# One encoder layer on one core: gate/up results split into halves as they are made, and a last block of 448 and 128 tokens

## The chip, the core and the metric

The kernel runs on one core of one Trainium2 chip. The metric is device time in microseconds (us). Before the change, three runs gave a median of 2537.41 us (2534.61 to 2539.2). The engines are TensorE (PE; its weight loads are listed apart as PEld), VectorE (DVE), ScalarE (ACT), GpSimd (POOL) and SyncE (SP), which here issues the DMAs of the stages that matter.

## What is computed

One layer of a streaming encoder on 576 tokens (64 of a running stream, 512 of a new one), width 2048, feed-forward width 5632, in float32. Attention and its projections come first and are not touched. What follows, cut from the reference:

```python
x = x + mix @ lp['w_out']
h = rmsnorm(x, lp['norm_ffn_g'])
x = x + (jax.nn.silu(h @ lp['ffn_w_gate']) * (h @ lp['ffn_w_up'])) @ lp['ffn_w_down']
...
y_prompt = rmsnorm(xp[:, N_META:], final_norm_g)
y_sample = rmsnorm(xs, final_norm_g)
```

`rmsnorm` multiplies by 1/sqrt(mean(x*x) + 1e-6) and a gain.

## The kernel before

**Numbers.** Every float32 operand v is split into hi, a copy rounded to a faster matmul format (fp32r), made on ScalarE, and lo = v - hi, made on VectorE. A product is three matmuls: hi x hi, hi x lo, lo x hi. In the trace `wh`, `wl` are the halves of a weight tile and `bh`, `bl` those of an operand; almost all instructions of ScalarE and VectorE are recorded under line 125, through which they are issued.

**Seven products.** `winograd` (line 1068) multiplies a 2 x 2 arrangement of weight tiles by a 2 x 2 arrangement of operand quarters (128 rows x 288 tokens) with seven products instead of eight. Four of the seven weights are sums of tiles (`ws`, made by GpSimd at line 1095 or by VectorE); likewise operands 3 to 7 of a chunk are partly sums of quarters. Each product takes the first two kinds of matmul (line 1126) over all its chunks, then the third kind (line 1130). `take` then adds the PSUM bank into the result. `WIDE` and `CHAIN` (lines 1010 and 1012) are orders of the seven products; `step` is a hook called after each.

**Gate/up stage** (line 1280). 22 steps u, one per 256 columns of the feed-forward width, each a gate pass and an up pass of 7 products x 24 matmuls of 128 x 288. ScalarE applies silu (`gated`), GpSimd multiplies gate and up into w, computes four sums of its quarters, and SP stores w to `actspill` and the sums to `sumspill` in HBM.

**Down stage** (line 1428). The 22 chunks are consumed in `blocks` of 4, 4, 4, 4, 4 and 2. For each of the first five, eight column groups d of 256 output columns run `down_rows` (line 1358): one 1 MB weight load `raw` (two buffers), seven products of 12 matmuls in the order `CHAIN`, results added into the residual rows y0 to y15, which are loaded from `x2spill` two at a time in block 0. While a block runs, `builder` (line 1228) loads the next block's quarters, 144 KB each, four ahead, and splits each: a copy `bh` on ScalarE, a subtraction `bl` on VectorE, 28 of each for a block, 8 for the last. The first block's operands are loaded and split by the same builder in the last steps of the last up pass.

**Last block** (2 chunks, 8 operands, no sums). Two halves of 288 tokens; in each, eight column groups load their weights (512 KB), split them and multiply (`plain_rows`, line 1338; its matmuls are recorded at line 205). `squares` (line 1372) squares each finished y on GpSimd and accumulates (lines 1376 to 1380), and ScalarE scales y by the final gain. `finish` (line 1383) sums the squares over partitions by a matmul with ones (line 1406), takes the reciprocal root, transposes y back on TensorE (line 1394), multiplies, and stores twelve groups `ot`; the first half's runs between the column groups of the second, the second half's at the end.

SP issues loads and stores in one queue, in the order in which the scheduler placed them; a transfer whose buffer is not free holds up those behind it.

Of the kernel before, what the change touches and what calls it, by code (L numbers as in the profile page):

```python
# [2 lines left out]

# [128 lines left out]
def encoder_step(  # L132
# [196 lines left out]
    sumspill = dp.tile([FC // 2, P, 4, QH], F32, name="sumspill")  # L329
    mspill = dp.tile([KC, P, TQ], F32, name="mspill")  # L330
# [673 lines left out]
    rb2 = rw.tile([P, TQ], F32, name="rb2")  # L1004
    sq2 = rw.tile([P, TQ], F32, name="sq2")
# [13 lines left out]

    def operand(m, p, src):  # L1020
        hi = bc.tile([P, QH], F32R, name=f"bh{p}_{m}")
        lo = bc.tile([P, QH], F32R, name=f"bl{p}_{m}")
        pin(S.activation(hi, src, AF.Copy))
        pin(V.tensor_tensor(lo, src, f32(hi), op=ALU.subtract))
        operands[m, p] = (hi, lo)
# [41 lines left out]

    def winograd(wpool, spool, raws, slots, take, banks=None, engine=V, step=lambda: None, stag=("ws", 3),
# [10 lines left out]
        def split_weights(n, srcs):  # L1079
            wh = wpool.tile([P, n, P], F32R, name="wh", tag="wh", bufs=2)  # L1080
            wl = wpool.tile([P, n, P], F32R, name="wl", tag="wl", bufs=2)
# [104 lines left out]
    close_ma()  # L1186
    fb, close_fb = pool("fb", "right")


    def stile():  # L1190
        return fr.tile([P, QH], F32, name="s", tag="s", bufs=4)

    def combined(c11, c12, c21, c22, chain):
# [15 lines left out]
        def take(p, banks):  # L1209
            if p == 1:  # L1210
                s[1] = stile()
                S.activation(s[1], banks[1], AF.Copy)
            elif p == 6:
                s[2] = stile()
# [13 lines left out]
    def builder(m0, count, plain, ahead, by_product=False):  # L1228

        srcs = {}  # L1230
        for m in range(m0, m0 + count):
            quarter = [actspill[2 * m + f, :, c] for f in range(2) for c in (slice(0, QH), slice(QH, TQ))]
            if plain:
                for p, src in zip((1, 2, 4, 5), quarter):
                    srcs[m, p] = src
            else:
                for p, src in zip(ORDER, (quarter[0], quarter[2], sumspill[m, :, 2], sumspill[m, :, 0],
                                          sumspill[m, :, 1], quarter[3], sumspill[m, :, 3])):
                    srcs[m, p] = src
        order = [p for p, _ in CHAIN]  # L1240
        todo = sorted(srcs, key=lambda mp: order.index(mp[1])) if by_product else list(srcs)

        def fetch(n):
            for m, p in todo[n:n + 1]:
                hi = bc.tile([P, QH], F32R, name=f"bh{p}_{m % 8}")
                lo = bc.tile([P, QH], F32R, name=f"bl{p}_{m % 8}")
                load(f32(lo), srcs[m, p])
                operands[m % 8, p] = (hi, lo)

        for n in range(ahead):  # L1250
            fetch(n)
        for n, (m, p) in enumerate(todo):
            fetch(n + ahead)
            hi, lo = operands[m % 8, p]
            pin(S.activation(hi, f32(lo), AF.Copy))
            yield
            pin(V.tensor_tensor(lo, f32(lo), f32(hi), op=ALU.subtract))
            yield
# [17 lines left out]

    turn = 0
    norm = token_norm()
    start = builder(0, blocks[0], False, 4, True)
    for u in range(FC // 2):  # L1280
        out = {}
        for which, wsrc in (("g", w_gate), ("u", w_up)):
# [9 lines left out]
            take = combined(*quarters(c[:, 0, :], c[:, 1, :]), chain)  # L1292
            done = [0]

            def step():
                if u == 0 and which == "u":
                    next(norm, None)
                if u == FC // 2 - 1 and which == "u":
                    done[0] += 1
                    if done[0] > 2:  # L1300
                        for _ in range(2 * blocks[0]):
                            next(start, None)

            if first:
                winograd(fw, fb, raws, range(4, 8), take, banks0, step=step)
            else:
                winograd(fw, fb, raws, range(8), take, step=step, chain=chain)
# [4 lines left out]
        if u == 0:  # L1312
            gated(g)
        for f in range(2):
            G.tensor_tensor(w[:, f, :], w[:, f, :], g[:, f, :], op=ALU.mult)
            if u < FC // 2 - 1:
                store(actspill[2 * u + f], w[:, f, :])
        if u < FC // 2 - blocks[-1]:
# [6 lines left out]
            store(sumspill[u], t)  # L1325
    for _ in start:
        pass
    for f in range(2):
        store(actspill[FC - 2 + f], out["u"][:, f, :])
    close_fb()  # L1330
    close_rw()
    yy, close_yy = pool("yy", "right")
    close_fw()
    yp, close_yp = pool("yp")

    y = []

    def plain_rows(m0, n, d, hs, slots, done):

        banks = {(f, h): pmt()[:, 0:QH] for f in range(2) for h in hs}  # L1340
        r = load_raw(fr, w_down, m0 * 256, 2 * n, d * 256, 2)
        for g in range(0, n, 2):
            for f in range(2):
                wh = yp.tile([P, 4, P], F32R, name="wh", tag="wh", bufs=2)
                wl = yp.tile([P, 4, P], F32R, name="wl", tag="wl", bufs=2)
                split(wh, wl, r[:, 2 * g:2 * g + 4, f * P:(f + 1) * P])
                for k in range(4):
                    m = slots[g + k // 2]
                    ops = [operands[m, ((1, 2), (4, 5))[k % 2][h]] for h in hs]
                    mm3([banks[f, h] for h in hs], wh[:, k, :], wl[:, k, :], [o[0] for o in ops],  # L1350
                        [o[1] for o in ops], g + k == 0, g + k == n + 1)
        for f in range(2):
            for h in hs:
                c = y[2 * d + f][:, h * QH:(h + 1) * QH]
                V.tensor_tensor(c, c, banks[f, h], op=ALU.add)
                done(2 * d + f, h)

    def down_rows(m0, n, d, slots, step):
        raws = [load_raw(fr, w_down, m0 * 256, 2 * n, d * 256, 2)]
        y11, y12, y21, y22 = quarters(y[2 * d], y[2 * d + 1])  # L1360
# [6 lines left out]
        winograd(yp, yp, raws, slots, take, step=step, chain=CHAIN)  # L1367

    tok = [[(0, NS), (NS, P), (192, 96)], [(QH, P), (416, P), (544, 32)]]
    sqs = {}  # L1370

    def squares(i, h):
        c = y[i][:, h * QH:(h + 1) * QH]
        if i == 0:
            sqs[h] = stile()
            G.tensor_tensor(sqs[h], c, c, op=ALU.mult)
        else:
            t = stile()
            G.tensor_tensor(t, c, c, op=ALU.mult)
            G.tensor_tensor(sqs[h], sqs[h], t, op=ALU.add)  # L1380
        S.activation(c, c, AF.Copy, scale=gE[:, i:i + 1])

    def finish(h, ahead):
# [4 lines left out]
        groups = [(q, j) for q in range(4) for j in range(3)]  # L1388

        def turned(q, j):  # L1390
            o, n = tok[h][j]
            ps = pmt()
            for k in range(4):
                PE.transpose(ps[0:n, k * P:(k + 1) * P], y[q * 4 + k][:, o:o + n], ident)
# [7 lines left out]
        vc = yp.tile([P, 3], F32, name=f"vc{h}")  # L1402
        rc = yp.tile([P, 3], F32, name=f"rc{h}")
        V.memset(vc, 1.0)
        for j, (o, n) in enumerate(tok[h]):
# [128 lines left out]
```

## Time and profile before

| | us |
|---|---|
| median of 3 runs | 2537.41 |
| the profiled execution | 2533.22 |
| its span | 2531.3 |
| attention | 0 to 853 |
| output projection | 853 to 970 |
| gate/up | 970 to 1961.9 |
| down, blocks 0 to 4 (with the step into it) | 1961.9 to 2447.1 |
| last block and outputs | 2447.1 to 2531.3 |

The profile shows the profiled execution alone, and its times are counted from the span's start; the time of that execution is 1.92 us longer than the span. Busy times are sums over instructions. Matmuls overlap, so the pace of TensorE is read from the starts of successive matmuls or from a stretch in which it never waits. In the lists of waits, "A <- B" says that A was held up by B. "PEclk" or granted clock is the TensorE clock as a share of full speed.

### The profile page before, as it was taken

Reading aid. Unit: us, or ns where it says so; the run is one execution under the profiler, and the core shown is the slowest. Engines: PE = TensorE matmul, PEld = TensorE weight load, DVE = VectorE, ACT = ScalarE, POOL = GpSimd, SP = SyncE. Lnnn points to the kernel's source line nnn. Section 1 sums busy time; section 2 is a strip of 40 time slices with the busy share of each in tenths; the row PEclk is TensorE's granted clock in tenths of the full one; section 3 lists DMA queues with packets and bytes.
Section 4 is the critical chain, followed back from the end, with each engine's and each line's share of the span. In section 5 each row is a group of like instructions: output and inputs, shape, how many; then the busy total and the mean of one; then the engine's idle time right before and its main releaser. Section 6 shows DMA issues by size and latency. Waiting matters only on the chain. (4 is left out here: it accounts for less than half of the span.)

```text
span 2531.3 us, 44872 instructions
## 1 busy us (share of the span) xinstructions
PE 2440.7 (96%) x17847; PEld 2381.8 (94%) x17847; DVE 1800.2 (71%) x2826; ACT 1106.6 (44%) x2008; POOL 744.3 (29%) x621
## 2 busy tenths in 40 slices
PE   8999999989999999999999999999999899999997
PEld 6999999988999888999999999999999899999997
DVE  5555555556555568877777777777777899999975
ACT  5343333333433444444444444444445444444445
POOL 0000000010000265644545454454543222222236
PEclk9999999999999999999999999999999899999999
DMA  7432232334322553333433333333335642542334
GB/s 216 141 93 80 81 87 83 82 111 120 100 84 76 166 151 112 125 126 121 137 109 117 117 125 132 119 125 100 128 128 167 207 150 84 159 157 84 111 100 150
DMA packets 330116, 307.73 MB, mean 122 GB/s; under 512 B 24708, under 2 KB 298507, under 8 KB 329907
## 3 DMA queue, kind: packets, MB, share of 16 engines
q1 hardware_dynamic: 329346, 302.80, 38.3%
q8 instruction: 140, 2.29, 0.4%
q0 software_dynamic: 560, 2.06, 0.2%
q14 instruction: 70, 0.57, 0.1%
HBM read 250.82 MB, written 56.68 MB: 121 GB/s over the span
## 5 line engine op out<-in xcount | busy, mean ns | idle before, releaser
L1126 PE MATMUL m<-bh,wh 128*128 128x288 f32 x3584 | 968.0, 296 | 11.0 <-DMA bl<-sumspill 8.4
L1126 PE MATMUL m<-bl,wh 128*128 128x288 f32 x3584 | 967.5, 295 | 0.0
L1126 PEld LDWEIGHTS m<-bh,wh 128*128 128x128 f32 x3584 | 673.9, 188 | 11.8 <-ACT wh L125 11.7
L1126 PEld LDWEIGHTS m<-bl,wh 128*128 128x128 f32 x3584 | 677.4, 189 | 0.1
L1130 PE MATMUL m<-bh,wl 128*128 128x288 f32 x3584 | 585.5, 298 | 17.1 <-DVE wl L125 14.5
L1130 PEld LDWEIGHTS m<-bh,wl 128*128 128x128 f32 x3584 | 512.2, 188 | 30.6 <-DVE wl L125 30.1
L1095 POOL TENSOR_TENSOR ws<-raw 128x512 f32<-128x512 f32 x256 | 344.1, 1352 | 599.1 <-DVE wl L125 319.2
L125 ACT ACTIVATE wh<-ws 128x512 fp32r<-128x512 f32 (+1 forms) x340 | 288.8, 849 | 447.6 <-PE m L1126 296.8
L125 DVE TENSOR_TENSOR wl<-ws,wh 128x512 fp32r<-128x512 f32 (+1 forms) x340 | 378.8, 1114 | 114.3 <-ACT wh L125 114.3
L125 DVE TENSOR_TENSOR wl<-raw,wh 128x512 fp32r<-128x512 f32 x416 | 403.7, 984 | 26.1 <-ACT wh L125 16.8
L125 ACT ACTIVATE wh<-raw 128x512 fp32r<-128x512 f32 x416 | 249.7, 626 | 306.2 <-PE m L1126 279.9
L108 PE MATMUL ps<-xh,wh 128*128 128x296 f32 x960 | 221.4, 312 | 1.2 <-ACT wh L125 1.2
L108 PE MATMUL ps<-xh,wl 128*128 128x296 f32 x960 | 210.7, 301 | 1.2 <-DVE wl L125 1.2
L108 PE MATMUL ps<-xl,wh 128*128 128x296 f32 x960 | 210.5, 301 | 0.0
L108 PEld LDWEIGHTS ps<-xh,wh 128*128 128x128 f32 x960 | 157.1, 191 | 5.5 <-ACT wh L125 1.7
L108 PEld LDWEIGHTS ps<-xh,wl 128*128 128x128 f32 x960 | 157.0, 190 | 2.2 <-DVE wl L125 2.2
L125 DVE TENSOR_TENSOR y<-y,m 128x288 f32<-128x288 f32 x312 | 139.6, 447 | 27.2 <-PE m L1130 18.0
L108 PEld LDWEIGHTS ps<-xl,wh 128*128 128x128 f32 x960 | 157.5, 190 | 0.0
L125 DVE TENSOR_TENSOR ws<-ws,raw 128x512 f32<-128x512 f32 x128 | 92.3, 722 | 83.6 <-POOL ws L1095 77.2
L125 DVE TENSOR_TENSOR wl<-wr,wh 128x1024 fp32r<-128x1024 f32 (+1 forms) x110 | 117.7, 1070 | 36.9 <-ACT wh L125 35.4
L125 ACT ACTIVATE wh<-wr 128x1024 fp32r<-128x1024 f32 (+1 forms) x110 | 101.7, 929 | 61.8 <-PE ps L108 52.0
L1273 POOL TENSOR_TENSOR c<-c,rb 128x576 f32<-128x576 f32 x44 | 73.2, 1664 | 164.8 <-ACT c L125 162.3
(359 smaller groups left out, 3342.5 us busy)
## 6 DMA issues: line engine op xcount, KB each, us to landing
raw<-in_ffn_w_gate SPq DMA_DIRECT2D x44, 1024.0 KB, 6.9
raw<-in_ffn_w_up SPq DMA_DIRECT2D x44, 1024.0 KB, 5.9
raw<-in_ffn_w_down SPq DMA_DIRECT2D x40, 1024.0 KB, 5.4
wr<-in_w_in SPq DMA_DIRECT2D x60, 512.0 KB, 4.0
actspill<-c SPq DMA_DIRECT2D x44, 288.0 KB, 2.1
sumspill<-c SPq DMA_DIRECT2D x20, 576.0 KB, 2.8
bl<-sumspill SPq DMA_DIRECT2D x80, 144.0 KB, 3.5
bl<-actspill SPq DMA_DIRECT2D x68, 144.0 KB, 3.9
```

The lines of the kernel that those rows point to most:

```text
L108: self.tc.keep_in_program_order(self.pe.matmul(out, lhsT, rhs, start=start, stop=stop))
L125: ins = issue(*args, **kwargs)
L1095: engine.tensor_tensor(w[:, k:k + m, :], pick(xs), pick(ys), op=op)
L1126: PE.matmul(banks[p], wh[:, k, :], x, start=first and new and k == 0 and x is hi, stop=False, skip_group_check=not new)
L1130: PE.matmul(banks[p], wl[:, k, :], hi, start=False, stop=last and k == n - 1, skip_group_check=not new)
L1273: G.tensor_tensor(g[:, f, :], g[:, f, :], rb2, op=ALU.mult)
```

## The change

1. **Gate/up.** For u = 2 to 19 nothing goes to `actspill` or `sumspill`. In the steps of u + 1 (the last three of the gate pass, the first four of the up pass) `parts` splits each of the chunk's seven operands: a one-column ScalarE copy into the tile's first column, whose source is a column of the result that the product just ended has produced; the hi copy over the whole tile; the lo subtraction on VectorE; and one store of both halves (288 KB) to `partspill`. Chunks 0 and 1 (`WHOLE`) and the last two are stored as before.
2. **Down.** `fetch_parts` loads both halves of an operand with one 288 KB load, and nothing is split in blocks 0 to 3 but the operands of chunks 0 and 1, which `starter` splits in the last up pass and at its end. Block 4 still splits the last block's 8 operands. Weight pools of gate/up and down are one, with four tiles of each half in flight in the down stage instead of two.
3. **The step into the down stage.** The first weights, y0 and y1 are requested from the last up pass on (SP in program order there), the last gate x up multiplication is done by quarters on GpSimd, y2 to y4 take a buffer of gate/up's weights, and y5 to y15 are all requested in the first block's second column group.
4. **Last block.** Its tokens are cut into part 0 (448: 288 and 160) and part 1 (128). Weights are loaded and split once and kept. Squares are taken by ScalarE; GpSimd only accumulates them, and not part 1's last three. `finish` of part 0 makes 20 output groups between part 1's column groups; that of part 1 makes 4.

How it moves instructions, at three places. First ScalarE in the gate/up stage, in the second half of a gate pass: `c<-m` takes a product's result, `wh` are copies of weights to come. Before:

```order
785 L125 ACTIVATE wh<-raw 128x512
786 L125 ACTIVATE wh<-ws 128x1024 x2
787 L125 ACTIVATE c<-m 128x288
788 L125 ACTIVATE wh<-ws 128x1024
789 L125 ACTIVATE c<-m 128x288
790 L125 ACTIVATE wh<-ws 128x1024
```

Now:

```order
885 L125 ACTIVATE c<-m 128x288
886 L125 ACTIVATE parts<-c 128x1
887 L125 ACTIVATE parts<-c 128x288
888 L125 ACTIVATE wh<-ws 128x1024
889 L125 ACTIVATE c<-m 128x288
890 L125 ACTIVATE parts<-c 128x1
891 L125 ACTIVATE parts<-c 128x288
892 L125 ACTIVATE wh<-ws 128x1024
893 L125 ACTIVATE c<-m 128x288
894 L125 ACTIVATE wh<-raw 128x512 x6
```

Ahead of the weight copies at these places stand a one-column copy and a hi copy.

Second, VectorE in the third block of the down stage, in the fifth column group (its rows of y are `y_22271`, `y_22273` before and `y_22248`, `y_22250` now). Before:

```order
2006 L125 TENSOR_TENSOR y_22271<-y_22271,m 128x288
2007 L125 TENSOR_TENSOR wl<-ws,wh 128x512
2008 L125 TENSOR_TENSOR y_22273<-y_22273,m 128x288
2009 L125 TENSOR_TENSOR bl_6_24528<-bl_6_24528,bh_6_24527 128x288
2010 L125 TENSOR_TENSOR wl<-raw,wh 128x512
2011 L125 TENSOR_TENSOR y_22271<-y_22271,m 128x288
2012 L125 TENSOR_TENSOR wl<-ws,wh 128x512
2013 L125 TENSOR_TENSOR ws<-ws,raw 128x512
2014 L125 TENSOR_TENSOR y_22271<-y_22271,m 128x288
2015 L125 TENSOR_TENSOR bl_6_24573<-bl_6_24573,bh_6_24572 128x288
```

Now:

```order
2043 L125 TENSOR_TENSOR y_22248<-y_22248,m 128x288
2044 L125 TENSOR_TENSOR y_22250<-y_22250,m 128x288
2045 L125 TENSOR_TENSOR wl<-ws,wh 128x512 x2
2046 L125 TENSOR_TENSOR y_22248<-y_22248,m 128x288
2047 L125 TENSOR_TENSOR ws<-ws,raw 128x512
2048 L125 TENSOR_TENSOR y_22248<-y_22248,m 128x288
```

The subtractions `bl` are gone from between the weight halves and the additions into y.

Third, SP in block 0, up to the weights of the third column group (`raw_21968` before, `raw_22396` now). Before:

```order
577 L125 DMA y4_21964<-x2spill_68 128x576
578 L125 DMA y5_21966<-x2spill_68 128x576
579 L125 DMA y6_22119<-x2spill_68 128x576
580 L125 DMA y7_22121<-x2spill_68 128x576
581 L125 DMA bl4_6_22207<-sumspill_70 128x288
582 L125 DMA y8_22271<-x2spill_68 128x576
583 L125 DMA y9_22273<-x2spill_68 128x576
584 L125 DMA bl6_6_22296<-sumspill_70 128x288
585 L125 DMA bl3_6_22340<-actspill_69 128x288
586 L125 DMA bl7_6_22382<-sumspill_70 128x288
587 L125 DMA bl1_7_22423<-actspill_69 128x288
588 L125 DMA raw_21968<-in_ffn_w_down 128x8x256
```

Now:

```order
660 L125 DMA y8_22248<-x2spill_68 128x576
661 L125 DMA y9_22250<-x2spill_68 128x576
662 L125 DMA y10_22252<-x2spill_68 128x576
663 L125 DMA y11_22254<-x2spill_68 128x576
664 L125 DMA y12_22256<-x2spill_68 128x576
665 L125 DMA y13_22258<-x2spill_68 128x576
666 L125 DMA y14_22260<-x2spill_68 128x576
667 L125 DMA y15_22262<-x2spill_68 128x576
668 L125 DMA b3_4_22280<-partspill_71 128x576
669 L125 DMA b2_5_22377<-partspill_71 128x576
670 L125 DMA b4_5_22394<-partspill_71 128x576
671 L125 DMA raw_22396<-in_ffn_w_down 128x8x256
```

All remaining rows y, and whole operands in place of quarters, now stand ahead of these weights.

The diff, cut to its core:

```diff
+    def weight_tiles(wpool, n):
+        if n == 8 or not spare:
+            both = [wpool.tile([P, 8, P], F32R, name=x, tag=x, bufs=2) for x in ("wh", "wl")]
+            if n == 8:
+                return both
+            spare.append([w[:, 4:8, :] for w in both])
+            return [w[:, 0:4, :] for w in both]
+        return spare.pop()
...
+    def fetch_parts(m, p):
+        load(f32(operand_tile(m % 8, p)), partspill[m, :, PIECE[p]])
+
+    def fetcher(m0, count):
+        n = 0
+        for m in range(m0, m0 + count):
+            for p in ORDER:
+                fetch_parts(m, p)
+                yield
+                n += 1
+                if n % 2 == 0:
+                    yield
...
+    def starter():
...
+        todo = [p for p, _ in CHAIN]
+        for i in range(len(todo) + 2):
+            if i < len(todo):
+                for m in range(blocks[0]):
+                    if m < WHOLE:
+                        fetch_whole(m, todo[i], whole(m, todo[i]))
+                    else:
+                        fetch_parts(m, todo[i])
+            if i > 1:
+                for m in range(WHOLE):
+                    split_in_place(m, todo[i - 2])
+            yield
...
+    WHOLE = 2
+
+    def parts(u, srcs):
+        for p in ORDER:
+            b = fb.tile([P, 2, QH], F32R, name="parts", tag="parts", bufs=2)
+            S.activation(b[:, 0, 0:1], (yield), AF.Copy)
+            S.activation(b[:, 0, :], srcs[PIECE[p]], AF.Copy)
+            V.tensor_tensor(b[:, 1, :], srcs[PIECE[p]], f32(b[:, 0, :]), op=ALU.subtract)
+            store(partspill[u, :, PIECE[p]], f32(b))
+        yield
...
             def step():
...
+                done[0] += 1
+                if pieces and (which == "u" or done[0] > 4):
+                    try:
+                        pieces.send(took[WIDE[done[0] - 1][0]][:, 0:1])
+                    except StopIteration:
+                        pieces = None
+                if ending:
+                    next(start)
...
-            store(sumspill[u], t)
+            if u < WHOLE:
+                store(sumspill[u], t)
+            else:
+                pieces = parts(u, [b11, b12, b21, b22] + [t[:, i, :] for i in range(4)])
+                next(pieces)
...
+    LATE = TQ - P
+    spans = [[(0, 0, QH), (1, 0, LATE - QH)], [(1, LATE - QH, QH)]]
...
+    def plain_weights(m0, n, d):
         r = load_raw(fr, w_down, m0 * 256, 2 * n, d * 256, 2)
+            kept[d, f] = wh, wl = [room(names, F32R)[:, 0:4 * P].rearrange("p (k c) -> p k c", k=4) for _ in range(2)]
+            split(wh, wl, r[:, :, f * P:(f + 1) * P])
...
+    def squares(i, part):
+        alone = i == 0 or part and i > KC - 4
+        t = room(names if alone else sums)
+        for c, at in token_pieces(i, part):
+            S.activation(t[:, at], c, AF.Square)
+            S.activation(c, c, AF.Copy, scale=gE[:, i:i + 1])
...
-                    for i in (2 * d, 2 * d + 1):
-                        y.append(yy.tile([P, TQ], F32, name=f"y{i}"))
-                        load(y[i], x2spill[i])
+                if bi == 0 and d == 1:
...
+                    for i in range(6, KC):
+                        accumulator(i, yy.tile([P, TQ], F32, name=f"y{i}"))
...
+            for d in range(KC // 2):
+                plain_weights(first, n, d)
+                plain_rows(d, 0, slots)
+            before = finish(0, 0)
+            for d in range(KC // 2):
+                plain_rows(d, 1, slots)
+                for _ in range(3):
+                    next(before, None)
+            for g in (before, finish(1, 4)):
+                for _ in g:
+                    pass
```

More of the change, by code (lines that the diff above doesn't have):

```diff
@@ L1 @@
+import itertools
 import math
@@ L1079, in split_weights @@
         def split_weights(n, srcs):
[L1080 to L1081 removed]
+            wh, wl = weight_tiles(wpool, n)
             k = 0
@@ new lines, in fetch_whole, with act_quarter, whole @@
+    def fetch_whole(m, p, src):
+        operand_tile(m % 8, p)
+        load(f32(operands[m % 8, p][1]), src)
+    def act_quarter(m, q):
+        return actspill[2 * m + q // 2, :, q % 2 * QH:(q % 2 + 1) * QH]
+    def starter():
+        def whole(m, p):
+            q = PIECE[p]
+            return act_quarter(m, q) if q < 4 else sumspill[m, :, q - 4]
+        todo = [p for p, _ in CHAIN]
[10 more added lines that the diff above has]
+            yield
@@ new lines, in plain_rows @@
+    def plain_rows(d, part, slots):
+        for f in range(2):
+            wh, wl = kept[d, f]
+            outs = [pmt()[:, 0:b - a] for _, a, b in spans[part]]
+            for k in range(4):
+                ops = [[x[:, a:b] for x in operands[slots[k // 2], ((1, 2), (4, 5))[k % 2][h]]]
+                       for h, a, b in spans[part]]
+                mm3(outs, wh[:, k, :], wl[:, k, :], [o[0] for o in ops], [o[1] for o in ops], k == 0, k == 3)
+            for c, pi in zip(token_pieces(2 * d + f, part), outs):
+                V.tensor_tensor(c[0], c[0], pi, op=ALU.add)
+            squares(2 * d + f, part)
@@ L1365, in take, with room, finish @@
                 V.tensor_tensor(c, c, banks[p], op=ALU.add)
[L1367 to L1376, printed above, removed]
-        else:
[L1378 to L1388, printed above, removed]
+        winograd(fw, fs, raws, slots, take, step=step, chain=CHAIN)
+    tok = [[(0, 96), (96, 96), (192, 96), (QH, 80), (QH + 80, 80)], [(LATE, P)]]
+    sqs = [[], []]
+    def room(names, dtype=F32):
+        return bc.tile([P, 2, QH], dtype, name=next(names)).rearrange("p a b -> p (a b)")
+    def squares(i, part):
[4 more added lines that the diff above has]
+            S.activation(c, c, AF.Copy, scale=gE[:, i:i + 1])
+        w = slice(0, P if part else LATE)
+        if alone:
+            sqs[part].append(t)
+        else:
+            G.tensor_tensor(sqs[part][0][:, w], sqs[part][0][:, w], t[:, w], op=ALU.add)
+    def finish(part, ahead):
+        groups = [(q, j) for q in range(4) for j in range(len(tok[part]))]
         def turned(q, j):
-            o, n = tok[h][j]
+            o, n = tok[part][j]
+            h = o // QH
             ps = pmt()
             for k in range(4):
-                PE.transpose(ps[0:n, k * P:(k + 1) * P], y[q * 4 + k][:, o:o + n], ident)
+                PE.transpose(ps[0:n, k * P:(k + 1) * P], y[q * 4 + k][h][:, o - h * QH:o - h * QH + n], ident)
             return ps
@@ L1444, in encoder_step @@
         else:
[L1445 to L1454 removed]
+            rest = [m for m in range(8) if m not in slots]
+            free = [f"b{p}_{m}" for m in rest[::-1][:2] for p in ORDER]
+            free += [f"b{p}_{m}" for m in slots for p in (3, 6, 7)]
+            free += [f"b{p}_{m}" for m in rest[:-2] for p in ORDER]
+            sums, free = itertools.cycle(free[0:3]), free[3:]
+            names, rows = iter(free[:-6]), itertools.cycle(free[-6:])
+            for d in range(KC // 2):
[9 more added lines that the diff above has]
+                    pass
         first += n
[L1456 removed]
+    close_fs()
+    close_fw()
     close_fr()
     close_yy()
+    close_rw()
     close_bc()
```

184 lines of the change are left out of this document (94 added, 90 removed).

## The prediction

> **What bounds the kernel now.** I began with the page's busy times, then cut the span into stages by windows, then asked what TensorE waits for in each. The page, and the windows of the four stages that the change touches (times from the span's start; columns: length, then busy time and recorded instructions of each engine, granted clock, DMA share, GB/s):
>
> ```profile
> span 2531.3 us, 44872 instructions
> PE 2440.7 (96%) x17847; PEld 2381.8 (94%) x17847; DVE 1800.2 (71%) x2826; ACT 1106.6 (44%) x2008; POOL 744.3 (29%) x621
> ...
> 1105.00:1910.00 805.00, 805.00 (x6053) 805.00 (x6052) 601.79 (x685) 352.54 (x541) 399.33 (x289) 1.00 0.36 121
> ...
> 1970.40:2068.70 98.30, 94.97 (x672) 92.37 (x673) 89.69 (x156) 45.67 (x86) 23.22 (x18) 0.96 0.51 166
> 2068.70:2164.10 95.40, 92.39 (x675) 89.61 (x674) 89.54 (x157) 44.90 (x85) 21.12 (x16) 1.00 0.42 132
> ...
> 2259.50:2355.70 96.20, 92.12 (x674) 89.55 (x674) 88.15 (x157) 44.73 (x85) 20.70 (x16) 1.00 0.37 115
> 2355.70:2447.10 91.40, 90.53 (x674) 89.34 (x673) 80.59 (x137) 37.56 (x64) 18.95 (x14) 1.00 0.30 92
> 2355.70:2404.00 48.30, 47.55 (x353) 46.70 (x352) 44.78 (x78) 20.83 (x37) 10.79 (x8) 1.00 0.33 99
> 2404.00:2447.00 43.00, 42.87 (x322) 42.55 (x321) 35.81 (x61) 16.62 (x27) 8.16 (x6) 1.00 0.27 84
> 2447.10:2513.50 66.40, 60.68 (x436) 56.65 (x435) 43.03 (x75) 38.38 (x71) 52.39 (x59) 1.00 0.49 149
> 2513.50:2531.30 17.80, 8.36 (x60) 6.89 (x57) 5.79 (x13) 8.71 (x13) 2.21 (x3) 0.80 0.42 147
> ```
>
> In gate/up (first window) TensorE never stops: 805.00/6053 = 0.133 us per matmul, with VectorE at 75%. A down block of 672 matmuls at that pace is 89.4 us, but the full blocks take 95.40 to 96.20 us, and there VectorE is busy 92 to 94%. In block 4 the operand splits stop half way; from 2404 on TensorE keeps its pace (43.00/322 = 0.134). So VectorE gates the first four blocks. The waits of TensorE (us in total, times, longest), from 970 to 2446, then from 2068.7 to 2447:
>
> ```profile
> PE m L1130 <- DVE wl L125: 14.5, 27, 1.5
> PE m L1126 <- DMA bl<-sumspill: 8.4, 1, 8.4
> ...
> PE m L1130 <- DVE wl L125: 9.3, 19, 0.7
> ```
>
> The one long wait is the step into the down stage. TensorE's timeline there, and the traffic around it:
>
> ```profile
> 1960.78 1.23 PE L1130 MATMUL m<-bh,wl 128*128 128x288 f32 x8
> 1970.45 0.61 PE L1126 MATMUL m<-bh,wh 128*128 128x288 f32 x1 [8.43 <-DMA bl<-sumspill]
> 1970.86 0.44 PE L1126 MATMUL m<-bl,wh 128*128 128x288 f32 x1
> 1971.10 0.44 PE L1126 MATMUL m<-bh,wh 128*128 128x288 f32 x1
> ...
> 1945.00:1970.00 25.00, 17.02 (x128) 16.78 (x127) 21.05 (x41) 15.86 (x37) 4.83 (x4) 0.88 0.93 288
> 1970.00:1980.00 10.00, 8.66 (x41) 8.32 (x42) 6.58 (x11) 3.88 (x8) 3.70 (x3) 0.61 0.93 310
> 1990.00:1995.00 5.00, 5.00 (x39) 5.00 (x39) 4.37 (x9) 2.29 (x5) 1.89 (x2) 1.00 1.07 390
> ```
>
> Gate/up ends at T = 1961.9; after 8.43 us of idling the matmuls come every 0.24 us, and the mean clock of 0.61 over 10 us means (1 - 0.61)/0.5 x 10 = 7.8 us at half speed, which costs 3.9 us.
>
> **The change part by part.** Sums are made against the profiled execution (span 2531.3 us, time 2533.22 us), 4.2 us under the median of 2537.41 us; the same difference is then applied to the median. About 0.2% (5 us) can be told from no change.
>
> *Blocks 1 to 3.* Their 28 splits each leave this stage. The rows of the splits and of their neighbours (busy, mean ns):
>
> ```profile
> L125 DVE TENSOR_TENSOR bl<-bl,bh 128x288 fp32r<-128x288 f32 x126 | 83.8, 667 | 3.0 <-ACT bh L125 3.0
> L125 ACT ACTIVATE bh<-bl 128x288 fp32r<-128x288 f32 x124 | 53.0, 429 | 7.8 <-DMA bl<-sumspill 7.6 <-DMA bl<-actspill 0.2
> L125 DVE TENSOR_TENSOR y<-y,m 128x288 f32<-128x288 f32 x312 | 139.6, 447 | 27.2 <-PE m L1130 18.0 <-PE m L205 7.7
> L125 DVE TENSOR_TENSOR wl<-raw,wh 128x512 fp32r<-128x512 f32 x152 | 130.2, 857 | 12.6 <-ACT wh L125 12.2
> ```
>
> VectorE loses 28 x 0.667 = 18.7 of 89.5 us a block, which leaves 74% of today's 95.40; and there are four weight tiles instead of two to run ahead in. What is late next is TensorE itself. 95.40, 95.40 and 96.20 become 3 x 89.4 + 0.8 = 269.0: 287.0 to 269.0, -18.0 (-12 if half of the loss had another cause, -19 with no wait left). Each fetch doubles to 288 KB, so a block reads 28 x 147 KB = 4.1 MB more: 132 GB/s becomes 132 + 4.1 MB/95.4 us = 175, well under what the step into the stage moved.
>
> *Gate/up.* 18 chunks x 7 operands add 126 subtractions on VectorE, 126 copies and 126 one-column copies on ScalarE, 126 stores on SP; the actspill and sumspill stores go. By the rows of the subtractions beside (0.447 to 0.667 us) VectorE gets 56 to 84 us more in 18 chunks: in the window above 601.79 becomes about 672, 84%. TensorE's pace hides it as long as the next weights' low halves arrive: a product lasts 24 x 0.133 = 3.19 us, and its low half is needed only after 16 of 24 matmuls. The new wait is in ScalarE's queue: a one-column copy waits for the result of the product just ended, and behind it stand the weight copies of the products to come. But this wait ends at a point at which TensorE has only begun the next product, whose weights are already split. I take +1 (0 to +8); without that cover it is a rival.
>
> *Transition and block 0.* Before, T to the end of block 0 took 106.8 us. Operands of m = 2, 3 now arrive split, those of m = 0, 1 in the order of use with two products of lead, and the first weights are requested before T. So the 8.43 us wait and its slow clock go: I take 0.5. But SP's order has a new risk. After T it must move product 4's operands (864 KB), raw 1 (1024), y2 to y4 (864), two stores (576), five operands (1440), y5 to y15 at once (3168), three operands (864), and only then raw 2 (1024): 9824 KB = 10.06 MB. Before, raw 2 stood behind y0 to y9 and half-size fetches, and was issued 14.3 us into the block; the other two rows are the landing of such a load and the first copy that needs it:
>
> ```profile
> 1984.78 0.38 SPq L125 DMA_DIRECT2D raw<-in_ffn_w_down  x1
> ...
> raw<-in_ffn_w_down SPq DMA_DIRECT2D x40, 1024.0 KB, 5.4
> ...
> L125 ACT ACTIVATE wh<-raw 128x512 fp32r<-128x512 f32 x152 | 95.6, 630 | 109.0 <-PE m L1126 91.6 <-DVE wl L125 8.8 <-DMA raw<-in_ffn_w_down 3.7
> ```
>
> At 339 GB/s, the middle of the 288 and 390 above, 10.06 MB take 29.7 us: raw 2 lands at T + 30. One weight copy (0.63) later TensorE can start the third column group, which it is free for at T + 0.5 + 2 x 11.2 = T + 22.9: it stands about 8 us (4 at 390, 13 at 288), and a gap of that size brought the half clock above, 3.9 us again. Block 0: 0.5 + 89.4 + 1 for small waits + 8 + 3.9 = 102.8: -4.0. The Trainium skill ("TensorE: Matmul & The Clock Gate", "What's actually happening") says that an idle window of about 3.4 us halves the clock for about as long again; the trace agrees that it halves, but shows 7.8 us of it; by the page the cost would be 1.7 us, and the block 2.2 us shorter.
>
> *Block 4.* It still splits its 8 quarters; 91.4 becomes 90.4: -1 (-2 to +1).
>
> *Last block.* Before, two halves of 288 tokens, paced by the squares on GpSimd, and a tail of 17.8 us. The rows:
>
> ```profile
> L1380 POOL TENSOR_TENSOR s<-s 128x288 f32<-128x288 f32 x30 | 28.2, 939 | 2.3
> L1379 POOL TENSOR_TENSOR s<-y 128x288 f32<-128x288 f32 x30 | 26.0, 867 | 9.4 <-DVE y L125 9.4
> L125 ACT ACTIVATE y<-y,gT 128x288 f32<-128x288 f32 x32 | 17.1, 535 | 22.9 <-POOL s L1379 22.3 <-POOL s L1376 0.4
> ...
> 603.90 0.28 PE L108 MATMUL sp<-kmh,qnl 128*128 128x144 f32 x1
> 604.02 0.27 PE L108 MATMUL sp<-rkh,rq0h 128*128 128x144 f32 x1
> 604.12 0.28 PE L108 MATMUL sp<-rkl,rq0h 128*128 128x144 f32 x1
> 604.24 0.28 PE L108 MATMUL sp<-rkh,rq0l 128*128 128x144 f32 x1
> ...
> 2513.50 2.78 PE L1394 MATMUL m<-ident,y 128*96 128x128 f32 x24
> 2516.12 0.28 PE L1406 MATMUL m<-ones,s 128*128 128x2 f32 x2
> ...
> 2515.53 1.28 ACT L125 ACT_TABLE_LOAD   x1
> 2517.97 1.28 ACT L125 ACT_TABLE_LOAD   x1
> 2520.14 1.26 ACT L125 ACTIVATE ot<-m,rc 128x512 f32<-128x512 f32 x2 [0.67 <-issue]
> ```
>
> A matmul of 144 columns still takes 0.112 us, so the cut into 288 + 160 and 128 pays three pieces where two full halves were two. Part 0: 16 row groups x 12 x (0.133 + 0.112) = 47.0. Part 1: 192 x 0.112 = 21.5, and 80 transposes of 0.109 (2.62/24) between them = 8.7. ScalarE has per column group, by the rows of 288, at most 4 squares and 4 scalings near 0.5 and two weight copies of 0.63 = 5.3 of part 0's 5.9 us: a close fit that may leave the last squares late, so I add 3 for part 1's wait on the sum of squares. The tail before: last matmul 2513.50, normalisers ready 2520.1, twelve groups of output until 2531.3. Now 4 groups of one part: 6.6 us to the normalisers less some 1.6, since the last add, square and sum are 128 wide instead of 288, and of the 11.2 us of output a third is 3.7, to which I add 0.7 for a last store that lands alone: 9.4. Together 89.6 against 66.4 + 17.8 = 84.2: +5.4 (0 to +9). The Trainium skill ("TensorE: Matmul & The Clock Gate", "Back-to-back issue gap") gives about 81 ns per matmul for 128 columns in sustained pairs with weight loads: part 1 would be 15.6 instead of 21.5, and the sum 6 us less. The rows above speak against it: 112 ns at 144 columns.
>
> Sum: -18.0 + 1 - 4.0 - 1 + 5.4 = -16.6: 2533.2 to 2516.6, and 2537.4 to **2521**.
>
> **The rivals.** *The transfers keep up.* If the queue runs at 390 GB/s or better, and nothing before T is left in it, raw 2 comes at T + 26 or sooner, and a shorter gap may leave the clock up. Then block 0 is 11.9 us shorter: 2509. For it speaks the 390 window; against it the two others. The Trainium skill ("HBM Reference", the figures at its head) says that a core streaming alone reaches about 425 GB/s; no window here shows that.
>
> *VectorE becomes the bound of gate/up (slower).* Blocks with VectorE at 94% lose (95.40 - 89.4)/56 = 0.107 us a product. If the anchors in ScalarE's queue, each behind a VectorE add in three of seven products, push weight copies late by as much in the 18 x 14 = 252 products of the chunks with new work, that is +27 instead of +1: 2547. It decides from 17.6/252 = 0.07 us a product, where all gain is gone. Against it: 84%, not 94%, and spare room between products; for it: in gate/up each weight split is one of 1024 columns.
>
> *The waits of the down stage have another source.* The recorded waits on wl from 2068.7 on are 9.3 us, of some 20 lost to 89.4; if half of the loss stays (spacing, not waits), blocks 1 to 3 give 9 less: 2530.
>
> **How the numbers follow.** Forecast 0.50, transfers keep up 0.25, half of the loss stays 0.15, VectorE bound 0.10. The time is the forecast's, 2521. The range goes down to the first rival with the last block's gain at its best (2509 - 5.4 = 2503) and up to the third with 4 us more of late transfers (2534); it leaves out the second rival and some of the ends, under 2 in 10. Faster by over 0.2% (below 2532): forecast, first and third rival but for their upper ends, 0.85; within: a half-size second rival, 0.07; slower (above 2542): 0.08.
>
> **What would show it.** In blocks 1 to 3: 89 to 90 us each, VectorE near 75%. At T: no wait over 1 us; in block 0 one wait on raw 2, ScalarE or GpSimd sums behind it, some 8 us, then half clock. Gate/up: 805 us of TensorE in 805, VectorE about 84%. Last block: 0.112 us in part 1, 47 us for part 0, some 9 after the last matmul. The prediction is wrong if gate/up stretches, if the wait in block 0 is missing (too high) or if blocks 1 to 3 stay above 92 us.

## The result, and the profile after

The changed kernel takes 2519.15 us (median of 4 runs, 2516.65 to 2521.25), the kernel before 2538.3 (4 runs, 2534.61 to 2539.68): a ratio of 0.9926, with a 95% interval of 0.9909 to 0.9944, so some 19 us less. The profiled execution has 2521.25 us and a span of 2519.5, 11.8 under the span of before. The page's head, then the windows of the stages, with the columns as before:

```profile
span 2519.5 us, 45585 instructions
PE 2445.7 (97%) x18045; PEld 2401.2 (95%) x18045; DVE 1774.4 (70%) x2826; ACT 1135.7 (45%) x2182; POOL 729.3 (29%) x588
```

```profile
1108.00:1913.00 805.00, 805.00 (x6052) 805.00 (x6052) 660.14 (x809) 432.44 (x792) 408.87 (x288) 1.00 0.41 140
...
1965.20:2070.70 105.50, 94.67 (x674) 93.68 (x673) 76.44 (x133) 34.69 (x62) 23.17 (x18) 0.94 0.69 234
2070.70:2160.60 89.90, 89.66 (x674) 89.25 (x673) 73.51 (x128) 32.35 (x57) 23.30 (x16) 1.00 0.55 186
2160.60:2250.50 89.90, 89.70 (x674) 89.29 (x673) 73.51 (x128) 32.40 (x57) 23.47 (x16) 1.00 0.56 186
2250.50:2340.50 90.00, 89.78 (x675) 89.37 (x674) 74.60 (x128) 32.80 (x58) 22.32 (x16) 1.00 0.55 177
2340.50:2430.00 89.50, 89.41 (x673) 89.21 (x673) 74.49 (x138) 35.45 (x66) 20.09 (x14) 1.00 0.31 95
```

TensorE is still never idle in this window of gate/up, with VectorE at 82% (75% before). Each of blocks 1 to 3 is now within 0.6 us of TensorE's own 89.4, and VectorE is at 82 to 83% of the shorter time. What is left to wait for in the down stage is all in block 0 (us in total, times, longest):

```profile
PE m L1143 <- ACT wh L125: 5.1, 1, 5.1
PE m L1143 <- DVE y L125: 4.9, 2, 3.9
PE m L1147 <- DVE wl L125: 0.8, 1, 0.8
```

The stages of the two profiled executions, from first matmul to first matmul (the step begins where the last matmul of gate/up ends, so that the wait before counts to it):

| stage | before, us | after, us | difference | forecast |
|---|---|---|---|---|
| to the first gate matmul | 970.6 | 973.6 | +3.0 | 0 |
| gate/up | 991.2 | 991.6 | +0.4 | +1 |
| step and block 0 | 106.9 | 105.5 | -1.4 | -4.0 |
| blocks 1 to 3 | 287.0 | 269.8 | -17.2 | -18.0 |
| block 4 | 91.5 | 89.5 | -1.9 | -1 |
| last block and outputs | 84.2 | 89.5 | +5.3 | +5.4 |

The first row is code that the change does not touch; this time came out anywhere from 970.6 to 976.2 in the profiles of this study, that of e5 aside. Block 0 also varies: with the same code in it, it took 102.6 to 105.5 us in six profiles. So the profiled pair shows less of the gain than the runs do.

The two places in block 0, in TensorE's timeline (the matmuls of one product start at each row; a column group is seven products):

```profile
1965.23 1.22 PE L1143 MATMUL m<-b,wh 128*128 128x288 f32 x8
...
1969.57 1.29 PE L1143 MATMUL m<-b,wh 128*128 128x288 f32 x8 [0.99 <-DVE y L125]
...
1974.43 1.22 PE L1143 MATMUL m<-b,wh 128*128 128x288 f32 x8
1980.09 2.26 PE L1143 MATMUL m<-b,wh 128*128 128x288 f32 x8 [3.91 <-DVE y L125]
1983.11 1.33 PE L1143 MATMUL m<-b,wh 128*128 128x288 f32 x8
...
1999.65 2.29 PE L1143 MATMUL m<-b,wh 128*128 128x288 f32 x8 [5.12 <-ACT wh L125]
```

and in those of SP, GpSimd and VectorE:

```profile
1967.90 0.38 SPq L125 DMA_DIRECT2D raw<-in_ffn_w_down  x1
...
1978.66 7.74 SPq L125 DMA_DIRECT2D y<-x2spill  x12
1986.83 1.89 SPq L125 DMA_DIRECT2D b<-partspill  x3
1989.13 0.38 SPq L125 DMA_DIRECT2D raw<-in_ffn_w_down  x1
```

```profile
1976.54 2.49 POOL L1112 TENSOR_TENSOR ws<-raw 128x512 f32<-128x512 f32 x2 [8.40 <-DMA raw<-in_ffn_w_down]
1999.02 1.27 POOL L1112 TENSOR_TENSOR ws<-raw 128x512 f32<-128x512 f32 x1 [19.99 <-DMA raw<-in_ffn_w_down]
```

```profile
1977.84 1.74 DVE L125 TENSOR_TENSOR ws<-ws,raw 128x512 f32<-128x512 f32 x1 [3.75 <-POOL ws L1112]
1979.51 0.44 DVE L125 TENSOR_TENSOR y<-y,m 128x288 f32<-128x288 f32 x1
```

The 8.43 us wait at the step is gone: the first matmul of the down stage follows the last of gate/up at once, at T = 1965.23. In what follows raw 1 and raw 2 are the weights of the second and the third column group. The gap of 5.12 us ahead of the third group is raw 2, issued at 1989.13 behind twelve transfers of y and three operands, and used from 1999 on. The gap of 3.91 us was not forecast: it stands before the last product of the first group. That product needs the PSUM bank that VectorE's addition at 1979.51 reads, and on VectorE this addition stands behind the second group's weight sum, which waits for GpSimd and raw 1. The smaller gap of 0.99 us, before the third product, is another matter: the addition that ends it, at 1968.99, stands on VectorE behind operand splits and weight halves.

### The profile page after: what moved, and what is told of

It reads as the page before. It is cut to its first block, busy times and chain, and to the rows that moved or that the text cites. A ratio compares the mean times of both kernels' runs of the same rounds, so it can differ in the third digit from the quotient of the medians.

```text
span 2519.5 us, 45585 instructions
## 1 busy us (share of the span) xinstructions
PE 2445.7 (97%) x18045; PEld 2401.2 (95%) x18045; DVE 1774.4 (70%) x2826; ACT 1135.7 (45%) x2182; POOL 729.3 (29%) x588
## 5 line engine op out<-in xcount | busy, mean ns | idle before, releaser
L1143 PE MATMUL m<-b,wh 128*128 128x288 f32 x7168 | 1051.0, 296 | 13.4 <-ACT wh L125 7.7
L1143 PEld LDWEIGHTS m<-b,wh 128*128 128x128 f32 x7168 | 986.8, 189 | 16.1 <-ACT wh L125 9.6
L1147 PE MATMUL m<-b,wl 128*128 128x288 f32 x3584 | 581.0, 297 | 3.0 <-DVE wl L125 3.0
L1112 POOL TENSOR_TENSOR ws<-raw 128x512 f32<-128x512 f32 x256 | 363.2, 1427 | 562.6 <-DVE wl L125 286.6
L1147 PEld LDWEIGHTS m<-b,wl 128*128 128x128 f32 x3584 | 515.1, 189 | 4.3 <-DVE wl L125 4.3
L125 ACT ACTIVATE wh<-raw 128x512 fp32r<-128x512 f32 x384 | 227.5, 625 | 300.2 <-PE m L1143 259.8
L125 DVE TENSOR_TENSOR wl<-raw,wh 128x512 fp32r<-128x512 f32 x384 | 355.0, 949 | 7.4 <-ACT wh L125 6.6
L125 DVE TENSOR_TENSOR y<-y,m 128x288 f32<-128x288 f32 (+1 forms) x328 | 141.4, 436 | 110.6 <-PE m L1147 75.2
L125 DVE TENSOR_TENSOR ws<-ws,raw 128x512 f32<-128x512 f32 x128 | 116.0, 910 | 74.2 <-POOL ws L1112 72.1
L1412 POOL TENSOR_TENSOR c<-c 128x576 f32<-128x576 f32 x42 | 73.8, 1756 | 85.8 <-DVE c L125 81.8
```

The costliest lines, as they stand in the source:

```text
L125: ins = issue(*args, **kwargs)
L1112: engine.tensor_tensor(w[:, k:k + m, :], pick(xs), pick(ys), op=op)
L1143: PE.matmul(banks[p], wh[:, k, :], x, start=first and new and k == 0 and x is hi, stop=False, skip_group_check=not new)
L1147: PE.matmul(banks[p], wl[:, k, :], hi, start=False, stop=last and k == n - 1, skip_group_check=not new)
```

## The experiments

Lengths of stages are from the first matmul of one to that of the next in each profile.

**e1: raw 2 ahead of the rows y.**

```diff
                 if bi == 0 and d == 1:
+                    fetch_raw(first, n, 2)
                     Q.ordered = False
```

> The change, but the weights of block 0's third column group are requested ahead of y5 to y15 instead of behind them. In the change block 0 took 105.5 us: two gaps before the last product of its first column group (0.99 and 3.91 us, VectorE standing on the sums of raw 1, which landed late), a gap of 5.12 + 0.80 us before its third group (raw 2), and half clock after each. Theory (place in SP's queue): about 4 MB less stand ahead of raw 2, some 12 us at 340 GB/s, so the second gap and its slow clock go and the first stays: block 0 takes 96 to 99 us. Rival (the transfers as a whole are the limit): the rows y that now come later hold up VectorE's additions instead, the gap moves to the third or fourth column group, and block 0 stays above 103 us.

Measured: 2512.06 us, ratio to before 0.9912 (0.9896 to 0.9929); block 0 95.97 us. The gap ahead of the third group is gone and the one before the last product of the first group stays, at 2.30 us, as the theory has it. But the fourth group's weights now stand behind the rows, and one product there took 2.9 us instead of 1.6: the rival is right about 1.3 us.

**e2: raw 1 ahead of the last product's operands as well.**

```diff
                 if ending:
+                    if done[0] == 7:
+                        fetch_raw(0, blocks[0], 1)
                     next(start)
...
-    fetch_raw(0, blocks[0], 1)
...
                 if bi == 0 and d == 1:
+                    fetch_raw(first, n, 2)
```

> As the first kernel, and raw 1 is requested ahead of the operands of the first block's last product, for which SP waits until TensorE has used their buffers. In the change raw 1 was issued 2.7 us after the end of gate/up and landed 8.5 us later. Theory: SP stands 2 to 4 us at the operands' buffers, raw 1 lands about 4 us sooner, before VectorE needs its sums, and the gaps of 4.9 us with their half clock go as well: block 0 takes 90 to 93 us, against 105.5. Rival (bandwidth): the operands of the last product, now behind a megabyte, come late instead, and block 0 stays above 96 us.

Measured: 2511.76 us, 0.9906 (0.9891 to 0.9921); block 0 96.48 us. The theory fails here. Raw 1 was issued at 1961.9 instead of e1's 1967.1, but the operands of the last product that ScalarE has to split came later by it (ScalarE stood 3.2 us for them), a wait of 1.10 and one of 1.70 us remained, and the wait in the fourth group's first product grew from 1.05 to 1.85 us. What was won at one place was paid at two others, so the rival holds.

**e3: the splits back in the down stage, with the deeper weight buffers kept.**

```diff
-    WHOLE = 2
+    WHOLE = 20
...
-                build = fetcher(first + n, blocks[bi + 1])
+                build = builder(first + n, blocks[bi + 1], 4, False)
```

(with False, `builder` takes the seven operands of a chunk from `actspill` and `sumspill` in the order `ORDER`.)

> The change, but chunks 2 to 19 are stored unsplit in the gate/up stage and split in the down stage again, 28 copies on ScalarE and 28 subtractions on VectorE a block; the shared pools with four weight tiles in flight and the last block stay as changed. Theory (VectorE's splits gate blocks 1 to 3): 94 to 96 us a block, VectorE at 92 to 94%. Rival (the deeper weight buffers took the waits away): 90 us a block as in the change. Gate/up goes back by 0.4 us at most, since TensorE hid the splits there.

Measured: 2525.64 us in one run; the windows of blocks 1 to 3:

```profile
2067.60:2159.60 92.00, 90.61 (x674) 89.37 (x674) 85.06 (x157) 41.72 (x85) 23.25 (x16) 1.00 0.45 136
2159.60:2252.60 93.00, 90.63 (x674) 89.39 (x673) 84.56 (x157) 41.61 (x85) 22.66 (x16) 1.00 0.44 135
2252.60:2344.70 92.10, 90.72 (x675) 89.48 (x674) 85.24 (x157) 41.81 (x85) 22.99 (x16) 1.00 0.42 131
```

92.4 us a block, between the two expectations: VectorE is again at 91 to 93%, but with four weight tiles in flight TensorE loses 3 us a block by it and not 6.

**e8: two weight tiles in flight instead of four, splits gone.**

```diff
-            spare.append([w[:, 4:8, :] for w in both])
             return [w[:, 0:4, :] for w in both]
```

> The change with two weight tiles of each half in flight in the down stage, as in the kernel before, instead of four. Theory (the splits were what cost): blocks 1 to 3 stay at 90 to 91 us. Rival (the depth is what gained): 93 to 96 us a block.

Measured: 2531.96 us in one run; blocks 1 to 3 took 91.70, 90.95 and 91.54 us, block 4 91.52. Also between the two. Together, blocks 1 to 3 in us:

| | splits in the stage | no splits |
|---|---|---|
| two weight tiles | 287.0 (before) | 274.2 (e8) |
| four weight tiles | 277.1 (e3) | 269.8 (the change) |

Undone alone, the splits cost 7.3 us of the change's blocks and the depth 4.4. Against the kernel before, either alone brings most of the gain (-12.8 without the splits, -9.9 with the depth), and the second adds what is left; but the kernel before differs from e3 and e8 in other things too, the order of its loads among them. That both work on the same lateness of the low halves is not shown: the kernel before has 8.9 us of recorded waits on low halves (`wl`) in these blocks, e8 has 0.6, and e3 has none, but 3.0 on additions into y and 1.1 on an operand copy.

**e4: the last block in two parts of 288.**

```diff
-    LATE = TQ - P
-    spans = [[(0, 0, QH), (1, 0, LATE - QH)], [(1, LATE - QH, QH)]]
+    LATE = QH
+    spans = [[(0, 0, QH)], [(1, 0, QH)]]
...
-    tok = [[(0, 96), (96, 96), (192, 96), (QH, 80), (QH + 80, 80)], [(LATE, P)]]
+    tok = [[(0, 96), (96, 96), (192, 96)], [(QH, 96), (QH + 96, 96), (QH + 192, 96)]]
```

> The change, but the last block is cut into two parts of 288 tokens instead of 448 and 128; weights are still split once and kept, squares still on ScalarE. In the change the last block took 89.5 us: 46.8 for part 0, 31.2 for part 1, 11.5 behind the last matmul. Theory (a matmul of 128 or 160 columns takes 0.112 us, one of 288 takes 0.133, so three pieces cost 17 us more than two): part 0 and part 1 take 25.6 us of matmuls each and part 1 has 48 transposes (5.2), the tail grows to about 17.5 for twelve groups: 74 to 76 us. Rival (ScalarE, with two weight copies, two squares and two scalings in 3.2 us a column group, becomes the bound): 80 us or more.

Measured: 2503.26 us, 0.9875 (0.986 to 0.9889); the last block takes 75.3 us against 89.5. In it and in the change (windows from its first matmul to the end; groups of its matmuls by shape in the change):

```profile
2427.40:2502.70 75.30, 67.20 (x512) 65.73 (x510) 32.61 (x69) 49.74 (x96) 22.23 (x27) 0.93 0.33 99
```

```profile
2430.00:2519.50 89.50, 80.71 (x692) 80.28 (x690) 33.76 (x85) 52.85 (x128) 22.74 (x27) 0.96 0.27 83
```

```profile
L205 PEld LDWEIGHTS m<-b,b 128*128 128x128 f32 x576 | 69.1, 190 | 0.0
L205 PE MATMUL m<-b,b 128*128 128x288 f32 x192 | 46.9, 333 | 0.0
L205 PE MATMUL m<-b,b 128*128 128x160 f32 x192 | 45.4, 236 | 0.0
L205 PE MATMUL m<-b,b 128*128 128x128 f32 x192 | 23.4, 276 | 0.0
```

The cut into 288, 160 and 128 needs 576 matmuls, each with its weight load, where 384 do; the 192 more cost their 0.11 us though they carry few columns. The tail behind the last multiplication grew from 11.5 to 18.5 us, and that is less than the 21 us saved ahead of it. ScalarE did not pace it: TensorE was busy for all of the first part's 25.7 us, ScalarE for 20.1.

**e11: e4 with the squares on GpSimd.**

```diff
-            S.activation(t[:, at], c, AF.Square)
+            G.tensor_tensor(t[:, at], c, c, op=ALU.mult)
```

> As e4 (two parts of 288 tokens, kept weights), but the squares are taken by GpSimd again, as in the kernel before. With ScalarE's squares the last block took 75.3 us. Theory (GpSimd's square and sum paced the block before, 2 x (0.867 + 0.939) = 3.6 us a column group, against 3.2 of TensorE): 16 groups lose 0.3 to 0.5 us each and the last sum comes late: 80 to 84 us. Rival (what gained was that the weights are split once): 75 to 77 us.

Measured: 2511.64 us (2 runs); the last block takes 82.1 us, 6.8 more than e4. The theory's size is right, its way not quite: part 0's matmuls did not slow down. TensorE ran ahead and then stood once for the sum and once for ScalarE behind it:

```profile
PE m L1523 <- POOL b L1495: 3.9, 1, 3.9
PE m L1509 <- ACT b L125: 2.2, 1, 2.2
```

So keeping the weights and moving the squares are worth 84.2 - 75.3 = 8.9 us together, of which the squares are 6.8 (that the kept weights are the other 2.1 is a difference, not a run); the cut into 448 and 128 takes 14.2 away again.

**e5 and e10: no one-column copies.**

```diff
-            S.activation(b[:, 0, 0:1], (yield), AF.Copy)
+            yield
```

> The change without the one-column copies ahead of the hi copies in the gate/up stage. Without them the hi copies stand closer together on ScalarE, in the last part of the gate pass, between the copies of the next weights, and no longer one behind each product. Theory (the column copy only sets the place, and the place matters): hi copies that wait for GpSimd's four sums hold up the weight copies behind them, TensorE waits on wh or wl in each of the 18 steps by 0.5 to 3 us, and gate/up takes 1000 to 1045 us instead of 991.6. Rival (the cover is wide enough for any place): 991 to 993 us, and the 126 one-column copies do nothing.

The first execution ran with TensorE at a granted clock of 0.222 over the whole span, attention included, and took 9933.98 us: nothing can be read from its stages. So it was run again:

> The kernel without the one-column copies once more, since its first execution ran at a granted clock of 0.22 from the attention stage on, which the edit does not touch. Theory (the column copy sets the place, and the place matters): gate/up takes 1000 to 1045 us instead of 991.6. Rival (the cover is wide enough for any place): 991 to 993 us. If the clock is at 0.2 to 0.3 again from the start, the kernel itself brings it about, and its stages say nothing of the copies.

Measured: 2558.93 us, ratio to before 1.0099 (1.0069 to 1.0128), at a clock of 0.991; gate/up takes 1027.6 us instead of 991.6. The hi copies on ScalarE from 1108 to 1913, without the column copies and with them (busy, mean ns, idle before and its releasers):

```profile
L125 ACT ACTIVATE parts<-c 128x288 fp32r<-128x288 f32 x119 | 52.6, 442 | 199.3 <-POOL c L1412 105.9 <-DMA partspill<-parts 60.5 <-POOL c L1420 32.8
```

```profile
L125 ACT ACTIVATE parts<-c 128x288 fp32r<-128x288 f32 x126 | 56.3, 446 | 4.0
L125 ACT ACTIVATE parts<-c 128x1 fp32r<-128x1 f32 x126 | 25.2, 200 | 28.4 <-DVE c L125 26.6
```

The waits of TensorE in gate/up without the column copies, from 990 to 2000:

```profile
PE m L1143 <- ACT wh L125: 11.9, 18, 1.7
PE m L1143 <- ACT c L125: 10.9, 15, 1.6
PE m L1147 <- DVE wl L125: 2.4, 3, 1.9
```

Without the anchor the copies stand where GpSimd has not yet multiplied gate and up (line 1412) or made the sums (line 1420) and the store has not freed the tile. ScalarE stands 199 us at them, and the weight copies and the copies of results behind them come late. The 126 column copies cost 25 us of ScalarE and save 36 us of gate/up.

**e6 and e7: two and three subtractions in place of each.**

```diff
             V.tensor_tensor(b[:, 1, :], srcs[PIECE[p]], f32(b[:, 0, :]), op=ALU.subtract)
+            V.tensor_tensor(b[:, 1, :], srcs[PIECE[p]], f32(b[:, 0, :]), op=ALU.subtract)
```

> The change with each of the 126 subtractions of the gate/up stage made twice. VectorE rises there from 660 to about 721 of 805 us (90%). Theory (TensorE's pace hides VectorE as long as it keeps up on average): gate/up stays at 991 to 994 us. Rival (waits begin before VectorE is full, as in the down stage of the kernel before, which lost 0.107 us a product at 92 to 94%): 1005 to 1020 us.

> The change with each of the 126 subtractions of the gate/up stage made three times. VectorE would stand at about 781 of 805 us (97%). Theory (cover until VectorE is full): near the end of the cover, 992 to 1005 us. Rival (the loss grows with the share, from 0.107 us a product at 92 to 94%): 252 products lose 0.15 us or more each, 1030 us or more.

Measured: 2559.87 and 2617.73 us, one run each; gate/up took 1034.8 and 1089.3 us, 43 and 98 more. The waits of TensorE from 990 to 2000 with two subtractions, then the window and ScalarE's column copies from 1108 to 1913 in that kernel:

```profile
PE m L1143 <- ACT c L125: 23.9, 16, 2.4
PE m L1147 <- DVE wl L125: 8.5, 11, 1.9
```

```profile
1108.00:1913.00 805.00, 776.12 (x5745) 767.93 (x5744) 705.52 (x887) 396.17 (x750) 406.25 (x272) 1.00 0.40 133
```

```profile
L125 ACT ACTIVATE parts<-c 128x1 fp32r<-128x1 f32 x119 | 24.0, 201 | 164.5 <-DMA partspill<-parts 90.7 <-DVE c L125 72.8
```

Both theories of a wide cover fall. The rival of e6 was too mild, that of e7 (1030 us or more) holds: with VectorE at 705.52 of 805, 88%, each of 252 products loses 0.17 us. The change, at 82%, lost nothing; so for work in this place the cover ended between the two. The copies of results on ScalarE became late (23.9 us), more than the low halves (8.5): the column copies ahead of them stood 164.5 us, against 28.4 in the change, 90.7 for the store that frees one of the two `parts` tiles and 72.8 for VectorE. With three subtractions it is the low halves that are late (55.1 us of waits in gate/up), and VectorE's share of the same window is 88% again (711.60 us): the stage stretches, and the share stays. So the 12% without work were not there to be filled. But it is not shown that VectorE's share as such sets the edge; the second subtraction also delays the store for which the anchor waits, and a run with more `parts` tiles was not made.

**e9: raws first, rows y two per group, and the last block of e4.**

```diff
                 if bi == 0 and d == 1:
+                    fetch_raw(first, n, 2)
...
-                    for i in range(6, KC):
+                if bi == 0 and 0 < d < 6:
+                    if d > 1:
+                        fetch_raw(first, n, d + 1)
+                    for i in (2 * d + 4, 2 * d + 5):
                         accumulator(i, yy.tile([P, TQ], F32, name=f"y{i}"))
```

> The change with two edits: in block 0 the weights of each column group from the third on are requested ahead of the rows y, and the rows y6 to y15 two per column group instead of all at once; and the last block in two parts of 288 tokens with kept weights (as e4). With raw 2 alone ahead of y5 to y15 block 0 took 96.0 us, and 1.3 us of waiting had moved to its fourth group, whose weights stood behind the rows. Theory (whatever must come first must stand first in SP's queue): the fourth group's gap goes, the one before the last product of the first group stays (3.3 us and its slow clock): block 0 takes 92 to 95 us, the last block 75: 2490 to 2496 us. Rival (the bytes of block 0 are the limit): block 0 stays at 96 us or above, the whole at 2497 us or above.

Measured: 2493.73 us (5 runs, 2493.01 to 2494.76), 0.983 of before (0.9817 to 0.9844): faster than both kernels. Block 0:

```profile
1963.70:2056.30 92.60, 89.69 (x675) 89.28 (x674) 75.94 (x133) 34.07 (x61) 24.40 (x18) 1.00 0.80 267
```

92.6 us at full clock, with waits of 1.31 and 1.59 us before two products of the first group and no other in the block. The theory holds for the times; of the 3.3 us with slow clock that it expected to stay in the first group, 2.9 us came, and the clock stayed up. The change's block was limited by the order of its transfers and not by their bytes: the same 24.7 MB go through in 12.9 us less, at 267 GB/s and not 234.

## Why the prediction was right, point by point

*Gate/up* (+1 forecast, +0.4): TensorE's pace hid the new work, as said, with VectorE at 660 us where 672 were worked out. But the bound of +8 and the 10% for the rival were given without knowing how near the edge is: e6 puts it before 88%. The rival named late weight copies behind the anchors. With more subtractions the anchors do hold up ScalarE (e6); in the change itself it is the other way round: without them weight copies come late and gate/up takes 36 us more (e10, 1.0099 of the kernel before). The prediction saw the one-column copy only as a new wait, not as what keeps the copies in place.

*Blocks 1 to 3* (-18.0, measured -17.2): the size was right, the reason half of it. The prediction put the loss on VectorE's share and named the four weight tiles beside it. e8, without the splits and with two tiles, has 12.8 of the 17.2, and by e3 a full VectorE costs half as much when the buffers are deeper. The third rival, that half of the loss stays, did not come: the blocks take 89.9 to 90.0 us, and no wait is recorded there. The lower end, -12 if half of the loss had another cause, does not follow from its own numbers: half of 18 is 9, as its third rival has it. Its share for VectorE, near 75%, was taken of the old 95.40 us; 70.8 of 89.9 would be 79%, and 82 to 83% were measured; what fills the difference no run shows.

*Step and block 0* (102.8 us forecast, 105.5 in this profile): the total is near, its terms are not, and that is luck. The wait of 8.43 us went, and the wait on raw 2 came, for the reason given: it was used at T + 34 instead of T + 30. It was 5.12 + 0.80 us and not 8, only because TensorE had already lost time before: it was free for the third group at T + 29.1 and not at T + 22.9. The step "1 for small waits" failed: raw 1 was taken to be in time. It landed at T + 11, about when its group was due, but on VectorE its sum stands ahead of an addition that the running group needs, and that cost 3.91 us and a stretch of half clock. The 0.99 us of the third product are not raw 1's: in e2, where raw 1 was issued before the end of gate/up, that wait is still 1.10. The rival "the transfers keep up" did not come, but e1 and e9 show that most or all of its 11.9 us were there to be had by order alone: 96.0 and 92.6, where the change's order gave 102.6 to 105.5.

*Block 4* (-1, measured -1.9): the remaining 8 splits no longer cost anything. With two weight tiles (e8) the block still took 91.5, so this gain is the depth's.

*Last block* (+5.4, measured +5.3): the narrow matmuls take 0.113 us (24 in the 2.72 us ahead of the last transposes), as the rows of 144 columns said. Part 0 took 46.8 us of 47.0 (2430.0 to 2476.8, 24 matmuls of 0.113 ahead of the first sum at 2479.48), part 1 31.2 of 21.5 + 8.7 + 3, so the wait that I added was not there; the tail took 11.5 and not 9.4, because 16 transposes and the sums stand behind the last multiplication. Two misses of 2 us cancelled, by luck.

The sum was -16.6 us to 2521; the runs gave 2519.15. In the profiled pair the stages that the change touches give -14.8 us. So the largest term, blocks 1 to 3, stands on its mechanism, and that the sum came within 2 us is in part luck, with two unforeseen gaps in block 0 against a smaller one at raw 2.

## What to carry to other kernels

Work moved under a bound engine is free only where it stands at the right place in its own engine's queue: the same copies were free behind a one-column anchor and cost 36 us without it, and twice the subtractions cost 43 us though VectorE was without work for 12% of the window. The anchor has a price of its own: what it waits for holds up everything behind it. Before bulk loads are requested all at once, look at what stands behind them in the queue; the rows y asked for all at once, ahead of raw 2, cost 7 to 10 us of block 0 (e1). And when a matmul of 128 to 160 columns takes hardly less than one of 288 (0.11 and 0.133 us here), count the pieces of a cut before the tail that it shortens.

## What the runs showed of the hardware

Half clock follows shorter gaps than the one of 8.43 us seen before. After the gap of 3.91 us the product starting at 1980.09 took 3.02 us instead of 1.59, and the next 1.70; from 1980.0 to 1984.8 the mean clock was 0.65. In e1 a gap of 2.30 us brought the same:

```profile
1978.90:1983.80 4.90, 4.83 (x25) 4.87 (x26) 3.15 (x6) 0.60 (x2) 0.00 (x0) 0.65 1.07 372
```

In e9, after a gap of 1.59 us, the clock stayed at 1.00:

```profile
1976.50:1979.80 3.30, 3.25 (x24) 3.28 (x25) 3.04 (x6) 0.53 (x2) 0.00 (x0) 1.00 1.03 391
```

But the length of the gap alone does not decide. In e2 the product after a gap of 1.85 us took 2.88 us instead of 1.59. In e6 two gaps of nearly the same length, before products of the same form, had different ends:

```profile
1439.09 2.35 PE L1143 MATMUL m<-b,wh 128*128 128x288 f32 x16 [2.32 <-ACT c L125]
1816.92 3.79 PE L1143 MATMUL m<-b,wh 128*128 128x288 f32 x16 [2.38 <-ACT c L125]
```

From 1438.8 to 1443.6 the clock was 1.00, from 1816.5 to 1821.5 it was 0.66. What else decides is open; a gap of 3.91 us or more brought half clock wherever it was looked at here. The window of e9 also shows 391 GB/s over 3.3 us, beside TensorE at full pace.

The execution of e5 shows a granted clock of 0.222 through a whole run of the same program that ran at 0.991 later; what brought it is open.
